# A decoder's linear attention: seven levels of scores as products of 32 columns, two halves of a projection moved, a bank counter set back

## The chip, the cores and the metric

The kernel runs on one core of a Trainium2 chip. The metric is the device time of one execution in microseconds (us), the median of several executions. Engines by their names in the profile: PE is the matrix engine (PEld its weight loads), DVE the vector engine, ACT the scalar engine, POOL the general engine, SP the queue that issues most DMAs. SBUF is the on-chip memory; PSUM is the matrix engine's result memory, here eight banks of 128 partitions by 512 float32.

## The reference

Two layers over 512 tokens of width 1024. Each layer is FFN, mixer, FFN, with a norm ahead of each part. The mixer of the first layer is the gated linear attention (GLA) that the change touches; that of the second is a stick-breaking attention (SB).

```python
for i in range(DEPTH):                      # DEPTH = 2, D_FF = 2816
    x = x + 0.5 * swiglu(rmsnorm(x, ffn1_norm[i]), ...)
    h = rmsnorm(x, mix_norm[i])
    y = gla_mixer(h, ...) if i % 2 == 0 else sb_mixer(h, ...)
    x = x + y
    x = x + 0.5 * swiglu(rmsnorm(x, ffn2_norm[i]), ...)
return rmsnorm(x, final_norm)
```

In GLA there are 4 heads with keys of 128 and values of 256. `b` is a running sum of log gates per key channel, and within a chunk

```python
diff = b_t[:, :, :, None, :] - b_t[:, :, None, :, :]
decay = jnp.exp(jnp.where(causal[:, :, None], diff, -jnp.inf))
scores = jnp.einsum('bhtk,bhtsk,bhsk->bhts', q_t, decay, k_t)
```

The decay depends on the key channel, so the scores are no plain product of q and k.

## The kernel before, in words

**Layout.** Tokens lie along the free axis (512 columns), features on the 128 partitions. A float32 product of full precision of the projections is made of three products of split operands (`mm3`, line 63 through `mm`): each weight tile is split by ACT (line 134, high part) and DVE (line 135, low part). Attention products are plain float32: the hardware does each as two passes, and the trace shows two weight loads and two matmuls for it.

**Order of the work.** Every projection is an `Entry` in one long queue, `feed`. `feed.step(1)` emits half of an entry of type `feat` (12 matmuls of 512 columns) or a quarter of one of type `tok`; `feed.entries(n)` emits whole ones. The GLA code calls `feed.step` between its own small steps, so that the projections fill the PE while DVE and ACT prepare the next attention step. A planner (the Tile framework's scheduler) then orders each engine's instructions by its own estimate; only inside a `manual_schedule` region is the order of an engine the written one among the region's own instructions.

**Banks.** PSUM banks have four tags: `a` (2 banks), `z` (3), `t` (2), `o` (1). Products without a tag take banks in the ring `aazzztto`; `turn_` counts on over the whole program. The products that close GLA and SB (`back`) use tags a, a, z, z for their first four accumulators and z, t, t, o for the last four.

**First FFN (lines 452 to 719).** Entries ahead of number `NORMED` multiply the raw input and scale the result afterwards (lines 672 and 679, one DVE operation per entry more). Between them, four pieces of `normed_input` scale and split the input itself, and from entry `NORMED` on that normed input (`nh`, `nl`) is used. Eight pieces `sums` follow until `sums_by`.

**Start of GLA (`run`, lines 1000 to 1046).** `two_halves` emits the first two projections (queries of heads 0 and 1, in the two `a` banks), `stats_a` the row statistics, `gate_low` 16 matmuls for the low-rank gate, `stats_b` the row scaling R (four small products, a DVE copy). Only with R can the two query products leave their banks (line 749). Then come `gate_logits`, and `feed.entries(2)`: the keys of heads 0 and 1, also with tag `a`.

**Levels (lines 850 to 905).** For each head the 128 by 128 score block of each of the four token tiles is built in S from a diagonal and seven levels B = 64, 32, ..., 1. `prepare(B)` makes from b a tile e (four DVE operations, lines 868 to 872, one exponential on ACT): in each group of 2B columns the first B hold keys with decay to the group's middle, the last B queries. Per level four products (128 weight columns, 96 for B = 32, 64 for B = 64; 64 moving columns) give all pairs, and a predicated copy with a mask (line 897, 64 columns for each of four tiles) puts the valid ones into S. A further product of k and q with 128 columns times the identity gives the diagonal (line 884). After each level one `feed.step`.

**Output (lines 907 to 989).** Transposed keys, three state products, S and state times values (`ps_o`), a square sum over the head's 256 values (`ps_on`, lines 967 to 969), a norm, and in `close` the product with the gate, split into `oh` and `ol` for `back`. The output of head h runs inside the levels of head h+1.

Of the kernel before, what the change touches and what calls it, by code (L numbers as in the profile page):

```python
# [10 lines left out]
F32 = mybir.dt.float32  # L11
F32R = mybir.dt.float32r
# [13 lines left out]
EPS = 1e-6  # L26
LEVELS = (64, 32, 16, 8, 4, 2, 1)
NEG = -1.0e30


@with_exitstack
def decoder(ctx: ExitStack, tc: tile.TileContext, a: dict, out: bass.AP):
# [29 lines left out]
    def mm(ps, l, r, first, last):  # L62
        st["pe"] = nc.tensor.matmul(ps, l, r, start=first, stop=last).ins  # L63
# [370 lines left out]
    def new_norm():  # L434
        st["h"], st["l"] = st["nh"], st["nl"]
# [16 lines left out]
    class FFN:  # L452
# [10 lines left out]
        def __init__(self, wg, wu, wd, gi, nxt, first=False, last=False):  # L463
            self.gi, self.normed, self.first = gi, False, first
            self.evac_g_, self.evac_u_ = self.evac_g, lambda ps: self.evac_u(ps, 0)
            if first:
                self.NORMED = 7
            self.defer, self.gates = [], []
# [253 lines left out]
    class GLA:  # L722
        def __init__(self, w_in, w_gk2, b_gk, og, w_out, nxt):
            self.w_in, self.w_gk2, self.b_gk, self.og = w_in, w_gk2, b_gk, og
            self.defer = []
            self.q, self.k, self.b, self.v = [None] * 4, [None] * 4, [None] * 4, []
            self.gn, self.on, self.hs = [None] * KD, [None] * KD, []
            chunks = [Chunk(cols(w_in, c * 256, 256), KD, 256) for c in range(4)]

            def qk(h):  # L730
                feat(chunks[h // 2], h % 2, lambda ps: self.evac_q(h, ps), "a", self.defer if h < 2 else None)

            def kk(h):
                feat(chunks[2 + h // 2], h % 2, lambda ps: self.evac_k(h, ps), "a")

            qk(0), qk(1), kk(0), kk(1), qk(2), qk(3), kk(2), kk(3)
            for c in range(4):
                tok(w_in, 1024 + c * 256, lambda i, ps, c=c: self.evac_v(c, i, ps), "a")
                ch = Chunk(cols(w_in, 2048 + c * 256, 256), KD, 256)
                for f in range(2):  # L740
                    feat(ch, f, lambda ps, j=2 * c + f: self.evac_g(j, ps), "a")
            back(w_out, 0, KD, self.hs, 1.0, nxt, late=2, tags=("a", "a", "z", "z", "z", "t", "t", "o"))
# [43 lines left out]
        def gate_weights(self):  # L786

            gr = self.ep.tile([P, KD, 16], F32, tag="gr", bufs=1, name="gr")
            with nc.allow_non_contiguous_dma("gate columns"):
                nc.gpsimd.dma_start(gr, cols(self.w_in, 3072, 16))  # L790
            self.gs = gs = self.ep.tile([P, KD, P], F32R, tag="gs", bufs=1, name="gs")
            nc.gpsimd.memset(gs.bitcast(F32), 0.0)
            nc.scalar.copy(gs[:, :, 0:16], gr)
            nc.vector.tensor_tensor(
                out=gs[:, :, 32:48], in0=gr, in1=gs[:, :, 0:16].bitcast(F32), op=ALU.subtract
            )
            w2 = self.gp.tile([P, T], F32, tag="g", name="w2")
# [12 lines left out]
            nc.gpsimd.dma_start(lf, a["c_lvl"])  # L810
            self.lvl = self.ep.tile([P, len(LEVELS) * P // 2], U8, tag="lvl", bufs=1, name="lvl")
            nc.vector.tensor_copy(self.lvl, lf)
            self.gf = self.gp.tile([P, T], F32, tag="g", name="gf")
# [3 lines left out]
        def gate_low(self):  # L817
            self.psg = psum("ps_gk", "z")
            for k in range(KD):
                mm(self.psg, self.gs[:, k], st["h"][k], k == 0, False)  # L820
                mm(self.psg, self.gs[:, k], st["l"][k], False, k == KD - 1)

# [27 lines left out]
        def levels(self, h):  # L850


            q, k, b = self.q[h], self.k[h], self.b[h]
            H = P // 2
            self.S[h] = S = self.hp.tile([P, NT, P], F32, tag="S", bufs=3, name="S")

            def four(t):
                return t.rearrange("p (n s) -> p n s", n=NT)

            def prepare(B):  # L860
# [3 lines left out]

                e = self.ep.tile([P, T], F32, tag="e", name="e")
                (b0, b1), (e0, e1) = halves(b), halves(e)
# [7 lines left out]

            def seconds(t, B):

                return t.rearrange("p (n m two c) -> p n m two c", n=NT, two=2, c=B)[:, :, :, 1, :]

            e = prepare(LEVELS[0])
            ps = psum("ps_S", "z")  # L880
            for i in range(NT):
                s = slice(i * P, (i + 1) * P)
                mm(ps[:, s], k[:, s], q[:, s], True, True)
            nc.vector.tensor_tensor(
                out=S, in0=four(ps), in1=ident.unsqueeze(1).to_broadcast([P, NT, P]), op=ALU.mult
            )
            yield
            for li in range(len(LEVELS)):
                e1 = prepare(LEVELS[li + 1]) if li + 1 < len(LEVELS) else None
                yield  # L890
                B = LEVELS[li]
                ps = psum("ps_S", "z")[:, 0 : T // 2].rearrange("p (n m c) -> p n m c", n=NT, c=B)

                R = P - B if B >= 32 else P
                for i in range(NT):
                    mm(ps[0:R, i], e[:, i * P : i * P + R], seconds(e, B)[:, i], True, True)
                nc.vector.copy_predicated(
                    out=seconds(S.rearrange("p n s -> p (n s)"), B)[0:R],
                    mask=self.lvl[0:R, li * H : (li + 1) * H]
                    .rearrange("p (m c) -> p m c", c=B)  # L900
                    .unsqueeze(1)
                    .to_broadcast([R, NT, H // B, B]),
                    data=ps[0:R],
                )
                e = e1

        def output(self, h):
# [57 lines left out]
            nc.scalar.copy(sh, sq)  # L965
            nc.vector.tensor_tensor(out=sl, in0=sq, in1=sh.bitcast(F32), op=ALU.subtract)
            ps = psum("ps_on", "o")
            mm(ps, self.one, sh, True, False)
# [31 lines left out]
        def run(self):  # L1000
            with ExitStack() as es:
# [5 lines left out]
                self.v = [vp.tile([P, D], F32, name=f"v{i}") for i in range(NT)]  # L1007
                self.S = [None] * 4
                new_norm()
                exp_ln_tables(st["silu"])  # L1010
# [34 lines left out]
                self.close(3)  # L1045
                feed.entries(self.end + 2 - feed.pos)


    class SB:
# [139 lines left out]
        def run(self):  # L1189
            with ExitStack() as es:  # L1190
# [19 lines left out]
                for s in range(17):  # L1210
# [16 lines left out]
                    else:  # L1227
                        feed.step(n)
                feed.entries(self.end + 2 - feed.pos)


# [255 lines left out]
```

## Time and profile before

| What | Value |
|---|---|
| median of 3 runs | 1815.3 us (1815.18 to 1816.06) |
| the profiled execution's own time | 1816.56 us |
| span of the profiled execution, first to last instruction | 1814.8 us |
| PE, DVE, ACT busy | 1794.2, 1473.1, 926.2 us |
| mean granted TensorE clock | 0.998 |
| first FFN | until about 340 us |
| GLA | about 346 to 577 us |

How to read it: timeline rows give start and duration in us, engine, line, operation, output and inputs, shape (for PE weight rows by weight columns, then the moving operand), how many were merged, and in square brackets the idle time of the engine before it with what ended it. Matmuls overlap in the pipeline, so the distance between starts, not the duration, tells what one costs. Busy time by stretch has PE, PEld, DVE, ACT, POOL, each with a count, then the granted clock.

### The profile page before, as it was taken

What the parts mean: (1) busy time and instruction counts of PE and PEld (TensorE: products, weight loads), DVE (VectorE), ACT (ScalarE), POOL (GpSimd) and SP (SyncE); (2) the same over time, 40 slices, a digit from 0 to 9 for tenths busy, and PEclk for the clock granted to TensorE, in tenths of its full rate; (3) what the DMA queues carried; (4) which work ended last, traced back from release to release, by engine and by line L of the source; (5) the groups of instructions that cost most, each with busy time, mean ns of one, the idle gap of its engine ahead of it and who ended that gap; (6) DMA issues with size and microseconds to landing.
All of it is one profiled execution on the core that took longest, in us unless ns stands there. A gap on an engine that the chain in (4) does not pass through costs nothing.

```text
span 1814.8 us, 28968 instructions
## 1 busy us (share of the span) xinstructions
PE 1794.2 (99%) x11806; PEld 1640.7 (90%) x11806; DVE 1473.1 (81%) x2373; ACT 926.2 (51%) x1455; POOL 8.5 (0%) x20
## 2 busy tenths in 40 slices
PE   9999999999999999999999999999999999999998
PEld 7899999889988899999989999999888788999997
DVE  7988887776877988887898888787888779888785
ACT  6444435445554544444554444455888844444444
POOL 0000000100000000000000000000000000000000
PEclk9999999999999999999999999999999999999999
DMA  6243333212223323332233333233221223333321
GB/s 210 72 131 112 105 117 114 84 51 67 70 70 102 107 94 112 113 125 84 82 119 119 110 116 106 89 96 96 70 71 59 70 93 116 105 105 105 120 90 70
DMA packets 177608, 179.09 MB, mean 99 GB/s; under 512 B 4098, under 2 KB 167988, under 8 KB 177476
## 3 DMA queue, kind: packets, MB, share of 16 engines
q1 hardware_dynamic: 176224, 175.13, 29.9%
q8 instruction: 92, 1.51, 0.3%
q0 software_dynamic: 576, 1.05, 0.2%
q10 hardware_dynamic: 676, 1.07, 0.2%
q14 instruction: 40, 0.33, 0.1%
HBM read 175.17 MB, written 2.10 MB: 98 GB/s over the span
## 4 chain that ended last, share of the span: by engine, by line
PE 85%; DVE 8%; ACT 4%; DMA 3%; issue 1%; DVEq 0%; ACTq 0%; SPq 0%
PE ps_d L63 23%; PE ps_w L544 14%; PE ps_f L63 14%; PE ps_z L544 9%; PE ps_q L544 9%; PE ps_t L63 4%; PE ps_b L63 3%; DVE wl L135 2%; PE ps_S L63 1%; DMA raw<-in_ffn_w_up_dram 1%; PE ps_bt L63 1%; PE ps_oT L1176 1%; PE ps_z L1114 1%; DMA raw<-in_ffn_w_gate_dram 1%; ACT wh L134 1%
## 5 line engine op out<-in xcount | busy, mean ns | idle before, releaser
L135 DVE TENSOR_TENSOR wl<-raw,wh 128x1024 fp32r<-128x1024 f32 x242 | 258.2, 1068 | 50.4 <-ACT wh L134 49.7
L134 ACT CAST wh<-raw 128x1024 fp32r<-128x1024 f32 (+1 forms) x242 | 223.8, 927 | 130.0 <-PE ps_f L63 43.4
L63 PE MATMUL ps_d<-hh,wh 128*128 128x512 f32 x672 | 254.7, 379 | 0.0
L63 PE MATMUL ps_d<-hh,wl 128*128 128x512 f32 x672 | 254.7, 379 | 0.0
L63 PE MATMUL ps_d<-hl,wh 128*128 128x512 f32 x672 | 254.7, 379 | 0.0
L134 ACT CAST wh<-s 128x1024 fp32r<-128x1024 f32 x136 | 142.3, 1046 | 115.0 <-PE ps_q L544 82.0
L135 DVE TENSOR_TENSOR wl<-s,wh 128x1024 fp32r<-128x1024 f32 x136 | 165.8, 1219 | 23.9 <-ACT wh L134 22.7
L63 PE MATMUL ps_f<-xh,wh 128*128 128x512 f32 x456 | 178.7, 392 | 3.4 <-DVE x L243 1.7
L63 PE MATMUL ps_f<-xh,wl 128*128 128x512 f32 x456 | 173.8, 381 | 0.4 <-DVE wl L1366 0.4
L63 PE MATMUL ps_f<-xl,wh 128*128 128x512 f32 x456 | 173.6, 381 | 0.0
L309 DVE SCALAR_TENSOR_TENSOR x<-ps_d,x 128x512 f32<-128x512 f32 x184 | 124.6, 685 | 59.8 <-PE ps_d L63 59.7
L544 PE MATMUL ps_z<-th,wh 128*128 128x256 f32 x544 | 150.1, 276 | 0.3 <-DVE u L555 0.2
L544 PE MATMUL ps_w<-nh,wl 128*128 128x256 f32 x544 | 149.6, 275 | 0.0
L544 PE MATMUL ps_w<-nl,wh 128*128 128x256 f32 x544 | 149.6, 275 | 0.0
L544 PE MATMUL ps_z<-th,wl 128*128 128x256 f32 x544 | 149.6, 275 | 0.0
L544 PE MATMUL ps_z<-tl,wh 128*128 128x256 f32 x544 | 149.6, 275 | 0.0
L544 PE MATMUL ps_w<-nh,wh 128*128 128x256 f32 x544 | 149.5, 275 | 0.0
L134 ACT CAST wh<-rawd 128x1024 fp32r<-128x1024 f32 x84 | 88.0, 1048 | 120.4 <-PE ps_d L63 100.7
L63 PEld LDWEIGHTS ps_d<-hl,wh 128*128 128x128 f32 x672 | 127.0, 189 | 18.0
L63 PEld LDWEIGHTS ps_d<-hh,wl 128*128 128x128 f32 x672 | 127.2, 189 | 16.5
L63 PEld LDWEIGHTS ps_d<-hh,wh 128*128 128x128 f32 x672 | 127.2, 189 | 16.5
L135 DVE TENSOR_TENSOR wl<-rawd,wh 128x1024 fp32r<-128x1024 f32 x84 | 102.6, 1222 | 34.7 <-ACT wh L134 34.4
(268 smaller groups left out, 4711.0 us busy)
## 6 DMA issues: line engine op xcount, KB each, us to landing
raw<-in_ffn_w_gate_dram SPq DMA_DIRECT2D x43, 1024.0 KB, 5.1
raw<-in_ffn_w_up_dram SPq DMA_DIRECT2D x43, 1024.0 KB, 5.1
rawd<-in_ffn_w_down_dram SPq DMA_DIRECT2D x84, 512.0 KB, 3.5
raw<-in_gla_w_in_dram SPq DMA_DIRECT2D x12, 1024.0 KB, 5.3
raw<-in_sb_w_in_dram SPq DMA_DIRECT2D x16, 512.0 KB, 3.8
raw<-in_gla_w_out_dram SPq DMA_DIRECT2D x4, 1024.0 KB, 5.1
raw<-in_sb_w_in_dram SPq DMA_DIRECT2D x4, 1024.0 KB, 5.0
raw<-in_sb_w_out_dram SPq DMA_DIRECT2D x4, 1024.0 KB, 4.9
```

The lines of the kernel that those rows point to most:

```text
L63: st["pe"] = nc.tensor.matmul(ps, l, r, start=first, stop=last).ins
L134: nc.scalar.copy(h, r).ins,
L135: nc.vector.tensor_tensor(out=l, in0=r, in1=h.bitcast(F32), op=ALU.subtract).ins,
L309: nc.vector.scalar_tensor_tensor(out=x, in0=back_by(ps, 4), scalar=0.5, in1=x, op0=ALU.mult, op1=ALU.add)
L544: nc.tensor.matmul(pairs(o), l_, r_, start=first and j + n == 0, stop=j == 3 and n == 2, skip_group_check=True)
L1114: nc.tensor.matmul(o_, l_, r_, start=first, stop=last, skip_group_check=True)
L1176: nc.tensor.matmul(po[e * 64 : e * 64 + 64, j * P : T], self.v[j][:, c : c + 64], self.wt[p, e][bk][:, c0 : c0 + n], start=j == 0, stop=j ...
```

## The change

1. **Levels.** All seven `prepare` calls come first (seven e tiles in buffers of their own, one `feed.step` after each and one more), then one region of PE products in written order. Each product has 32 weight columns and writes 32 partitions of PSUM; neighbours in the order go to different groups of 32 columns of the array. Levels 64 and 32 give blocks off the diagonal (16 products a head, moving columns 64 or 32), the diagonal and levels 16 to 1 only the four 32 by 32 blocks of each tile (16 products with 32 and 80 with 16 moving columns): 112 products a head for 32.
2. **Evacuation.** The blocks off the diagonal go straight to S by three ACT copies; the rest is gathered in a tile C of 32 columns a tile by one DVE product and five predicated copies of 16 columns a tile, and four DVE copies put C on S's diagonal. S is two lasting tiles, zeroed once by POOL.
3. **First keys.** The keys of head 0 take a `z` bank; half of that entry is emitted ahead of `stats_b`, half behind the query evacuations.
4. **Ring.** `turn_` is set to 0 at the end of GLA and of SB.
5. **Smaller edits.** `NORMED` of the first FFN is 8 for 7; `output` has one more yield ahead of `ps_on`, and the steps after it change so that the same number is taken; the gate columns are made in two tiles, the masks are folded to 16 columns a level by small DVE operations, and a folded identity is made.

```diff
+FINE = LEVELS[2:]
...
             if first:
-                self.NORMED = 7
+                self.NORMED = 8
...
             def kk(h):
-                feat(chunks[2 + h // 2], h % 2, lambda ps: self.evac_k(h, ps), "a")
+                feat(chunks[2 + h // 2], h % 2, lambda ps: self.evac_k(h, ps), "a" if h else "z")
...
-            self.S[h] = S = self.hp.tile([P, NT, P], F32, tag="S", bufs=3, name="S")
+            S = self.S[h] = self.Ss[h % 2]
...
-                e = self.ep.tile([P, T], F32, tag="e", name="e")
+                e = self.ep.tile([P, T], F32, tag="le", bufs=7, name="e")
...
+            es = []
+            for B in LEVELS:
+                es.append(prepare(B))
+                yield
+            yield
+            coarse, fine = psum("ps_S", "z"), psum("ps_C", "z")
+            def tile_(ps, c0, j, l, r):
...
+                o = ps[j * 32 : j * 32 + 32, c0 : c0 + n]
...
+                nc.tensor.matmul(o, l, r, start=True, stop=True, skip_group_check=True)
+            with tc.manual_schedule(engines={mybir.EngineType.PE}):
+                for i in range(NT):
+                    c = i * P
+                    for j, (li, m, n) in enumerate(((0, 64, 64), (0, 64, 64), (1, 96, 32))):
+                        tile_(coarse, (0, 0, T // 2)[j] + i * n, j, es[li][:, c + j * 32 : c + j * 32 + 32], es[li][:, c + m : c + m + n])
+                    tile_(coarse, T // 2 + i * 32, 0, es[1][:, c : c + 32], es[1][:, c + 32 : c + 64])
+                for i in range(NT):
+                    for j in range(NT):
+                        c = slice(i * P + j * 32, i * P + j * 32 + 32)
+                        tile_(fine, i * 32, j, k[:, c], q[:, c])
+                for n, B in enumerate(FINE):
+                    for i in range(NT):
+                        for j in range(NT):
+                            c = slice(i * P + j * 32, i * P + j * 32 + 32)
+                            e = es[n + 2][:, c]
+                            r = e.rearrange("p (m two c) -> p m two c", two=2, c=B)[:, :, 1, :]
+                            tile_(fine, P + n * 64 + i * 16, j, e, r)
+            C = self.hp.tile([P, NT, 32], F32, tag="C", bufs=1, name="C")
             nc.vector.tensor_tensor(
-                out=S, in0=four(ps), in1=ident.unsqueeze(1).to_broadcast([P, NT, P]), op=ALU.mult
+                out=C,
+                in0=fine[:, 0:P].rearrange("p (n c) -> p n c", n=NT),
+                in1=self.eye.unsqueeze(1).to_broadcast([P, NT, 32]),
+                op=ALU.mult,
             )
...
-            for li in range(len(LEVELS)):
-                e1 = prepare(LEVELS[li + 1]) if li + 1 < len(LEVELS) else None
-                yield
...
-                for i in range(NT):
-                    mm(ps[0:R, i], e[:, i * P : i * P + R], seconds(e, B)[:, i], True, True)
+            for n, B in enumerate(FINE):
                 nc.vector.copy_predicated(
...
+            nc.scalar.copy(S[0:64, :, 64:P], coarse[0:64, 0 : T // 2].rearrange("p (n c) -> p n c", n=NT))
+            for m in (0, 64):
+                nc.scalar.copy(
...
+            for j in range(NT):
+                s = slice(j * 32, j * 32 + 32)
+                nc.vector.tensor_copy(S[s, :, s], C[s])
...
             nc.vector.tensor_tensor(out=sl, in0=sq, in1=sh.bitcast(F32), op=ALU.subtract)
+            yield
             ps = psum("ps_on", "o")
...
+                self.Ss = [vp.tile([P, NT, P], F32, name=f"S{i}") for i in range(2)]
+                for S in self.Ss:
+                    nc.gpsimd.memset(S, 0.0)
...
                 self.gate_low()
+                feed.step(1)
                 stats_b("t")
                 flush(self.defer)
+                feed.step(1)
                 self.gate_logits()
-                feed.entries(2)
+                feed.entries(1)
...
-                        for _ in prev:
-                            feed.step(1)
+                        for n, _ in enumerate(prev):
+                            if h < 3 or n == 0:
+                                feed.step(1)
...
                 feed.entries(self.end + 2 - feed.pos)
+                turn_[0] = 0
```

More of the change, by code (lines that the diff above doesn't have):

```diff
@@ L786, in gate_weights, with fold @@
         def gate_weights(self):
-            gr = self.ep.tile([P, KD, 16], F32, tag="gr", bufs=1, name="gr")
+            def fold(x, y):
+                nc.vector.tensor_tensor(out=x, in0=x, in1=y, op=ALU.add)
+            gr = self.ep.tile([P, KD, 16], F32, tag="e", name="gr")
             with nc.allow_non_contiguous_dma("gate columns"):
                 nc.gpsimd.dma_start(gr, cols(self.w_in, 3072, 16))
[L791 to L796, printed above, removed]
+            self.gs = []
+            for u in range(2):
+                gs = self.ep.tile([P, 4, P], F32R, tag="le", bufs=7, name="gs")
+                nc.gpsimd.memset(gs.bitcast(F32), 0.0)
+                r = gr[:, u * 4 : u * 4 + 4]
+                nc.scalar.copy(gs[:, :, 0:16], r)
+                nc.vector.tensor_tensor(
+                    out=gs[:, :, 32:48], in0=r, in1=gs[:, :, 0:16].bitcast(F32), op=ALU.subtract
+                )
+                self.gs += [gs[:, k] for k in range(4)]
             w2 = self.gp.tile([P, T], F32, tag="g", name="w2")
@@ L810, in gate_weights @@
             nc.gpsimd.dma_start(lf, a["c_lvl"])
-            self.lvl = self.ep.tile([P, len(LEVELS) * P // 2], U8, tag="lvl", bufs=1, name="lvl")
-            nc.vector.tensor_copy(self.lvl, lf)
+            n = len(FINE) * 16
+            by = lf[:, 2 * P // 2 :].rearrange("p (l j c) -> p l j c", j=NT, c=16)
+            fold(by[:, :, 0:2], by[:, :, 2:4])
+            fold(by[:, :, 0], by[:, :, 1])
+            self.lvl = self.ep.tile([P, n], U8, tag="lvl", bufs=1, name="lvl")
+            nc.vector.tensor_copy(self.lvl.rearrange("p (l c) -> p l c", c=16), by[:, :, 0])
+            ey = self.ep.tile([P, P], F32, tag="e", name="ey")
+            nc.vector.tensor_tensor(out=ey[:, 0:64], in0=ident[:, 0:64], in1=ident[:, 64:P], op=ALU.add)
+            self.eye = self.ep.tile([P, 32], F32, tag="eye", bufs=1, name="eye")
+            nc.vector.tensor_tensor(out=self.eye, in0=ey[:, 0:32], in1=ey[:, 32:64], op=ALU.add)
             self.gf = self.gp.tile([P, T], F32, tag="g", name="gf")
@@ L819, in gate_low @@
             for k in range(KD):
-                mm(self.psg, self.gs[:, k], st["h"][k], k == 0, False)
-                mm(self.psg, self.gs[:, k], st["l"][k], False, k == KD - 1)
+                mm(self.psg, self.gs[k], st["h"][k], k == 0, False)
+                mm(self.psg, self.gs[k], st["l"][k], False, k == KD - 1)
         def gate_logits(self):
@@ L853, in levels @@
             q, k, b = self.q[h], self.k[h], self.b[h]
-            H = P // 2
-            self.S[h] = S = self.hp.tile([P, NT, P], F32, tag="S", bufs=3, name="S")
-            def four(t):
-                return t.rearrange("p (n s) -> p n s", n=NT)
+            S = self.S[h] = self.Ss[h % 2]
             def prepare(B):
@@ L873, in prepare @@
                 return e
[L875 to L880, printed above, removed]
-            for i in range(NT):
-                s = slice(i * P, (i + 1) * P)
-                mm(ps[:, s], k[:, s], q[:, s], True, True)
+            es = []
[3 more added lines that the diff above has]
+            yield
@@ new lines, in levels @@
+            coarse, fine = psum("ps_S", "z"), psum("ps_C", "z")
+            def tile_(ps, c0, j, l, r):
+                n = 1
+                for d in r.shape[1:]:
+                    n *= d
+                o = ps[j * 32 : j * 32 + 32, c0 : c0 + n]
+                if len(r.shape) == 3:
+                    o = o.rearrange("p (m c) -> p m c", c=r.shape[2])
+                nc.tensor.matmul(o, l, r, start=True, stop=True, skip_group_check=True)
[16 more added lines that the diff above has]
+                            tile_(fine, P + n * 64 + i * 16, j, e, r)
@@ L884, in levels @@
+            C = self.hp.tile([P, NT, 32], F32, tag="C", bufs=1, name="C")
             nc.vector.tensor_tensor(
-                out=S, in0=four(ps), in1=ident.unsqueeze(1).to_broadcast([P, NT, P]), op=ALU.mult
-            )
-            yield
-            for li in range(len(LEVELS)):
-                e1 = prepare(LEVELS[li + 1]) if li + 1 < len(LEVELS) else None
[L890 to L895, printed above, removed]
-                    mm(ps[0:R, i], e[:, i * P : i * P + R], seconds(e, B)[:, i], True, True)
+                out=C,
+                in0=fine[:, 0:P].rearrange("p (n c) -> p n c", n=NT),
+                in1=self.eye.unsqueeze(1).to_broadcast([P, NT, 32]),
+                op=ALU.mult,
+            )
@@ L897, in levels @@
+            for n, B in enumerate(FINE):
                 nc.vector.copy_predicated(
-                    out=seconds(S.rearrange("p n s -> p (n s)"), B)[0:R],
-                    mask=self.lvl[0:R, li * H : (li + 1) * H]
+                    out=C.rearrange("p n (m two c) -> p n m two c", two=2, c=B)[:, :, :, 1, :],
+                    mask=self.lvl[:, n * 16 : n * 16 + 16]
                     .rearrange("p (m c) -> p m c", c=B)
                     .unsqueeze(1)
-                    .to_broadcast([R, NT, H // B, B]),
@@ L903, in levels @@
-                    data=ps[0:R],
-                )
-                e = e1
+                    .to_broadcast([P, NT, 16 // B, B]),
+                    data=fine[:, P + n * 64 : P + n * 64 + 64].rearrange("p (n m c) -> p n m c", n=NT, c=B),
+                )
+            nc.scalar.copy(S[0:64, :, 64:P], coarse[0:64, 0 : T // 2].rearrange("p (n c) -> p n c", n=NT))
+            for m in (0, 64):
+                nc.scalar.copy(
+                    S[m : m + 32, :, m + 32 : m + 64],
+                    coarse[m : m + 32, T // 2 : T // 2 + P].rearrange("p (n c) -> p n c", n=NT),
+                )
@@ L1229, in run @@
                 feed.entries(self.end + 2 - feed.pos)
+                turn_[0] = 0
     phases = []
```

## The prediction

> **What bounds the kernel now.** I read the page first, then busy time by stretch around GLA, then timelines.
>
> ```profile
> span 1814.8 us, 28968 instructions
> ...
> PE 1794.2 (99%) x11806; PEld 1640.7 (90%) x11806; DVE 1473.1 (81%) x2373; ACT 926.2 (51%) x1455; POOL 8.5 (0%) x20
> ```
>
> ```profile
> 45.00:55.00 10.00, 8.12 (x36) 6.47 (x36) 10.00 (x21) 8.38 (x14) 0.00 (x0) 1.00 0.00 0
> 346.00:376.00 30.00, 28.29 (x126) 22.50 (x125) 15.46 (x35) 11.51 (x18) 0.00 (x0) 0.94 0.23 76
> 376.00:410.00 34.00, 34.00 (x220) 31.06 (x219) 30.93 (x66) 12.61 (x20) 0.00 (x0) 1.00 0.27 85
> 410.00:560.00 150.00, 148.71 (x1005) 136.00 (x1004) 110.53 (x205) 76.83 (x127) 0.00 (x0) 1.00 0.20 66
> ```
>
> PE is busy 99% of the span, and within GLA's levels (376 to 560) 182.7 of 184 us: there a product that goes away shortens the run, as long as DVE keeps up. DVE has room on average (141.5 of 184), little in the first head (30.93 of 34). Two stretches differ: at 45 to 55 DVE is full and PE waits; at 346 to 376 PE waits and its granted clock falls to 0.94.
>
> **The change, part by part.** *Levels, removed.* What one level costs PE is read between two of the surrounding projection's matmuls.
>
> ```profile
> 382.65 0.38 PE L63 MATMUL ps_f<-xl,wh 128*128 128x512 f32 x1
> 382.96 0.68 PE L63 MATMUL ps_S<-e 128*64 128x64 f32 x8
> ...
> 383.89 0.38 PE L63 MATMUL ps_f<-xh,wl 128*128 128x512 f32 x1
> ...
> 386.05 0.38 PE L63 MATMUL ps_f<-xl,wh 128*128 128x512 f32 x1
> ...
> 387.18 0.38 PE L63 MATMUL ps_f<-xh,wl 128*128 128x512 f32 x1
> ...
> 389.34 0.38 PE L63 MATMUL ps_f<-xl,wh 128*128 128x512 f32 x1
> 389.56 1.00 PE L63 MATMUL ps_S<-e 128*128 128x64 f32 x8
> ...
> 390.67 0.38 PE L63 MATMUL ps_f<-xh,wl 128*128 128x512 f32 x1
> ```
>
> The projection's own pitch is 0.216 us: 387.18 and 389.34 are the second and the twelfth matmul of one step, ten pitches apart. From 389.34 to 390.67 lie two pitches and a level of 128 weight columns: 1.33 - 0.43 = 0.90 us for eight passes. The same sum gives 0.81 for the level B = 64 ahead of 383.89 and 0.70 for B = 32 ahead of 387.18. A head has five levels at 0.90, one at 0.70, one at 0.81, and the diagonal, also eight passes of 128 columns, at 0.90: 6.9 us; four heads 27.6 us.
>
> *Levels, added.* 112 products a head are 224 passes of 32 weight columns. The trace has no such pass; the nearest are the weight loads of the levels before, and SB's products in two groups of 64 columns.
>
> ```profile
> L63 PEld LDWEIGHTS ps_S<-e x224: 133/192/192, 383.0 to 519.7; 128*128 128x128 f32 x80, 128*64 128x64 f32 x16, 128*96 128x96 f32 x16
> ```
>
> ```profile
> 1447.35 0.38 PE L1161 MATMUL ps_T<-ident,r 128*128 128x128 f32 x2
> 1447.66 2.37 PE L1176 MATMUL ps_oT<-wt,w 128*64 128x512 f32 x16
> 1449.96 0.48 PE L63 MATMUL ps_b<-oh,wh 128*128 128x512 f32 x1
> ```
>
> A load of 64 columns takes 133 ns, one of 128 takes 192: 0.030 us for 32 columns. I take that as the pitch of 32-column passes within one column group; 16 moving columns are short beside it. Do passes of different groups overlap? The 16 passes of L1176 (four each with 512, 384, 256 and 128 moving columns; the row names the first shape) end within 2.30 us (1447.66 to 1449.96). A pass of 128 moving columns costs 0.11 (two in 0.38 us, one lasting 0.27), so one after another they would take 16 x 2.5 x 0.11 = 4.4 us: they run in pairs. I assume the same of four groups of 32. The busiest group has, a head, 8 passes with 64 moving columns (0.056 each, half of 0.11) and 8 with 32 for the blocks off the diagonal, 8 for the diagonal, 40 for the fine levels: 0.45 + 56 x 0.030 = 2.1 us.
>
> Going from the whole array to groups and back drains it: after the last transpose (1447.35 + 0.11) a start was due at 1447.57 and came at 1447.66. I count this 0.09 twice, 0.10 for the uncovered load on the way back (0.48 for the usual 0.38) and half as much on entry: 0.33 a head. With 0.4 for unevenness 2.8 us a head, 11.2 in all (bounds 2.4 and 3.4 a head). Gain **16.4 us** (14 to 18).
>
> *Evacuation.*
>
> ```profile
> L897 DVE COPY_PREDICATED S<-lvl,ps_S x28: 420/438/742, 384.0 to 520.1; 128x256 f32<-128x256 uint8 x20, 64x256 f32<-64x256 uint8 x4, 96x256 f32<-96x256 uint8 x4
> L884 DVE TENSOR_TENSOR S<-ps_S,ident x4: 674/682/684, 379.1 to 486.0; 128x512 f32<-128x512 f32 x4
> ```
>
> A head loses seven copies at 0.43 and one product at 0.68, 3.7 us of DVE. By the slope of the two rows (256 columns 0.43, 512 columns 0.68) one product of 128 columns, five copies of 64 and four of 128 cost 0.3 + 5 x 0.25 + 4 x 0.3 = 2.8. ACT's three copies a head, under 1.5 us, lie on an engine half idle. S is read several steps later, so I cost this at nothing; uncovered, it would be 3 us in a head.
>
> *First keys.*
>
> ```profile
> 356.70 1.13 PE L63 MATMUL ps_R<-dg,gT 128*128 128x128 f32 x8
> 359.43 0.49 PE L63 MATMUL ps_f<-xh,wh 128*128 128x512 f32 x1 [1.60 <-DVE q L749]
> 359.72 0.63 PE L63 MATMUL ps_f<-xh,wl 128*128 128x512 f32 x1
> ...
> 363.13 0.39 PE L63 MATMUL ps_f<-xh,wh 128*128 128x512 f32 x1
> ```
>
> The last of eight R passes starts at 357.56 (356.70 + 1.13 - 0.27), so the keys were due at 357.67 and start at 359.43: both `a` banks hold queries until line 749 has run. Then eight matmuls take 3.41 us (359.72 to 363.13) for 1.72: the granted clock halved behind the pause. Together 3.45 us. With a `z` bank, half of the keys (12 x 0.215 = 2.6 us) runs ahead of R and half behind it, which covers the copy of R and the two queries (2 us of DVE). Next late are the gate logits, some 2 us further down DVE and ACT; head 1's keys can fill that if the planner puts them there. Gain **3.2** (1.5 to 3.5). [...]
>
> *Ring.*
>
> ```profile
> 577.06 0.38 PE L63 MATMUL ps_f<-xh,wh 128*128 128x512 f32 x1
> 579.14 0.48 PE L63 MATMUL ps_f<-xh,wh 128*128 128x512 f32 x1 [1.70 <-DVE x L243]
> ```
>
> Behind GLA the second matmul was due at 577.28 and came at 579.14, 1.86 late. Counted through the code, the ring stands at 111 there, so the FFN's first product takes bank `o`, which `back` empties last (line 243). Set to 0, it takes the two `a` banks, empty long since. Next come the input's last tiles; 24 matmuls of first halves (5.2 us) cover them. Gain **1.8** (0 to 1.9). At SB's end the waits view has no such wait: nothing.
>
> *First FFN.*
>
> ```profile
> 53.47 0.48 PE L63 MATMUL ps_f<-nh,wh 128*128 128x512 f32 x1 [1.36 <-ACT nh L630]
> ...
> 54.69 0.48 PE L63 MATMUL ps_f<-nl,wh 128*128 128x512 f32 x1 [0.52 <-DVE nl L631]
> ...
> 58.03 0.48 PE L63 MATMUL ps_f<-nh,wl 128*128 128x512 f32 x1 [0.27 <-DVE wl L135]
> ```
>
> PE waits 2.15 us for the normed input, by starts against pitch 0.16 more each time, 2.6. One more raw entry gives DVE 24 x 0.215 = 5.2 us more, less an added operation of 0.7. But DVE is full, and the eight `sums` now share four entries for five, so some waiting may return there. Gain **2.0** (0 to 2.6).
>
> *Square sums.*
>
> ```profile
> 443.22 0.28 PE L63 MATMUL ps_t<-wh,xh 128*128 128x256 f32 x1
> 443.66 0.50 PE L63 MATMUL ps_on<-sh,one 128*128 128x512 f32 x1 [0.16 <-ACT sh L965]
> ```
>
> Due at 443.33, 0.33 late; the added yield puts a step ahead of it. Four heads: gain **1.0** (0 to 1.3).
>
> *New waits.* The block of 112 products waits for the seventh e tile, and the projections wait behind it on PE. In head 0 PE's 34 us shrink by some 4 to 30 and DVE's 30.93 by 0.9 to 30: level, so a wait of a microsecond is likely. On DVE the first `prepare` of the next head waits until the block has read its buffer (seven of seven are in use); weight splits stand behind it, made up to two entries ahead of their use. In the last head two projection halves (5.2 us) no longer lie behind `close(2)`; products of `back` on earlier heads can take their place. On POOL two more fills of 128 x 512 stand ahead of the gate columns' DMA, some 1 us of a load wanted only after the statistics; the mask folding is a few short DVE operations in that stretch. I take **2.0 us lost** (0 to 5).
>
> Sum: 16.4 + 3.2 + 1.8 + 2.0 + 1.0 - 2.0 = 22.4. The profiled execution took 1816.6 us (its span and 1.8 around it), 1.3 above the median of 1815.3. So 1794.2 for such an execution, and **1793** as the median.
>
> **The rivals.** *One pass at a time (0.14).* Four groups don't overlap as two did, or PE can't issue short passes faster than it loads: 224 x 0.030 + 0.33 = 7.05 us a head, 0.6 more than before in all. Only the other parts are left (6.0): 22.4 - 16.4 - 0.6 = 5.4, 1810. For it: no row shows four groups, or 16 moving columns. Against: L1176's pairs. [...]
>
> *Issue-bound passes, slower (0.06).* Each short pass costs what the shortest of this trace did, the 64-column level: (0.68 - 0.22)/7 = 0.066, the last lasting 0.22 or so. 224 x 0.066 + 0.33 = 15.1 us a head, 33 more than before: 1815 + 33 - 6 = 1842. It ends slower from the pitch at which four blocks take 27.6 + 6.0: (33.6 - 1.3)/896 = 0.036 us. Against it: those passes loaded 64 columns, twice as many.
>
> *Feeders late (0.12).* The products overlap, but DVE is late at each of four heads, a pause of 1.8 and as much in lost clock, as at 357.67: 4 x 3.5 = 14 lost for 2: 1805. For it: DVE's 30.93 of 34. Against: 110.5 of 150 behind it.
>
> *The block is cut (0.04).* The planner may put other matmuls between the products; each cut costs 0.33 us again, ten cuts a head 13 us: 1806.
>
> **How the numbers follow.** Forecast 0.64, rivals 0.14, 0.06, 0.12, 0.04. The bounds of the parts give the forecast 1788 to 1805. The range goes to 1810 to take in half of the first rival and both of the last: about 0.85. Faster by over 0.2% (3.6 us; smaller differences can't be told from none here): all but the slower rival and a few of the first one's cases, 0.91; same 0.03; slower 0.06.
>
> **What would show it.** Right: the tile products of a head end within 2.4 to 3.4 us; no clock under 1.00 at 346 to 376; no wait for line 243 behind GLA; less waiting for nh and nl in the first FFN; GLA shorter by some 20 us. Wrong: starts of neighbouring tile products 0.03 us or more apart, 7 us a block; PE idle ahead of the block for the e tiles; other matmuls within it; a new wait ahead of `back`.

## The result and the profile after

The changed kernel takes 1798.39 us (median of four runs, 1797.29 to 1800.27), the kernel before 1815.68 beside it (four runs, 1815.18 to 1817.24): a ratio of 0.9904, 95% interval 0.9887 to 0.9922, 17.3 us faster. The forecast was 1793.0 with a range of 1788 to 1810: the sign and the range held, and the time lies 5.4 us above the forecast.

The profiled execution took 1799.37 us for a span of 1797.6. First the page of the changed kernel, then busy time in the four stretches that the prediction read.

```profile
span 1797.6 us, 30262 instructions
...
PE 1776.5 (99%) x12446; PEld 1624.4 (90%) x12446; DVE 1466.9 (82%) x2387; ACT 927.1 (52%) x1468; POOL 9.6 (1%) x23
...
q8 instruction: 97, 1.59, 0.4%
```

```profile
45.00:55.00 10.00, 10.00 (x48) 8.77 (x47) 10.00 (x20) 7.38 (x12) 0.00 (x0) 1.00 0.00 0
346.00:376.00 30.00, 29.91 (x146) 24.51 (x145) 16.75 (x37) 11.94 (x19) 0.00 (x0) 1.00 0.30 99
376.00:410.00 34.00, 34.00 (x426) 31.41 (x425) 33.65 (x83) 18.46 (x33) 0.00 (x0) 1.00 0.21 66
410.00:560.00 150.00, 143.91 (x1484) 129.47 (x1483) 111.19 (x211) 81.99 (x140) 0.00 (x0) 0.99 0.23 75
```

The first two stretches are what the prediction asked for: PE no longer waits at 45 to 55 (10.00 for 8.12; what is left of that wait, 0.86 us, lies behind the stretch, at 57.84), hardly waits at 346 to 376 (29.91 for 28.29), and the clock there is 1.00 for 0.94. But in the levels PE, which had been busy for 148.7 of 150 us, now stands still for 6.1 of 150. The waits view of GLA (376 to 566) names it:

```profile
PE ps_C L905 <- issue: 4.5, 2, 2.3
PE ps_t L64 <- DVE gn L775: 0.9, 1, 0.9
PE ps_b L64 <- DVE on L1029: 0.4, 1, 0.4
```

No e tile is waited for. Twice PE waits inside a block of tile products "for nothing that the profile shows" (issue). The timeline of PE shows a block without that (head 2) and one with it (head 1); each row is a group of passes, 224 a block.

```profile
465.28 0.85 PE L905 MATMUL ps_S<-e 128*32 128x64 f32 x31
...
466.25 1.57 PE L905 MATMUL ps_C<-e 128*32 128x16 f32 x160
467.75 0.48 PE L64 MATMUL ps_f<-xh,wh 128*128 128x512 f32 x1
```

```profile
426.82 1.42 PE L905 MATMUL ps_C<-e 128*32 128x16 f32 x142
430.45 0.36 PE L905 MATMUL ps_C<-e 128*32 128x16 f32 x18 [2.21 <-issue]
```

Head 2's block runs from 465.28 to 467.75: 2.47 us for 224 passes, close to the busiest group's 2.1 of the sum. Head 1's stops after 206 of its 224 passes, for 2.4 us from start to start (428.05 to 430.45). Head 3's stops after 177, also for 2.4 us, and the clock is halved behind it:

```profile
504.16 1.14 PE L905 MATMUL ps_C<-e 128*32 128x16 f32 x113
507.56 0.84 PE L905 MATMUL ps_C<-e 128*32 128x16 f32 x47 [2.26 <-issue]
508.32 0.80 PE L64 MATMUL ps_f<-xh,wh 128*128 128x512 f32 x1
...
511.04 0.38 PE L64 MATMUL ps_f<-xh,wh 128*128 128x512 f32 x1
```

From 508.32 to 511.04 lie six pitches of 0.216, so 1.3 us were due and 2.7 passed.

The table splits each profiled execution at the starts of four matmuls of the timeline: the first of the input's first FFN, the gate's first (`ps_gk`), the first behind GLA's last product (`ps_f` behind `ps_b`), and the first that reads that FFN's normed input (`nh`).

| us | to the first product | first FFN, up to the gate | gate and GLA | behind GLA, to `nh` | rest | span |
|---|---|---|---|---|---|---|
| before | 8.65 | 344.05 | 224.36 | 34.96 | 1202.76 | 1814.78 |
| after | 9.20 | 342.22 | 210.02 | 33.17 | 1202.95 | 1797.56 |
| difference | +0.55 | -1.83 | -14.34 | -1.79 | +0.19 | -17.22 |

### The profile page after: what moved, and what is told of

Its sections match the earlier page's. It is cut to its first block, busy times and chain, and to the rows that moved or that the text cites. A ratio compares the mean times of both kernels' runs of the same rounds, so it can differ in the third digit from the quotient of the medians.

```text
span 1797.6 us, 30262 instructions
## 1 busy us (share of the span) xinstructions
PE 1776.5 (99%) x12446; PEld 1624.4 (90%) x12446; DVE 1466.9 (82%) x2387; ACT 927.1 (52%) x1468; POOL 9.6 (1%) x23
## 3 DMA queue, kind: packets, MB, share of 16 engines
q8 instruction: 97, 1.59, 0.4%
## 4 chain that ended last, share of the span: by engine, by line
PE 87%; DVE 7%; ACT 4%; DMA 1%; issue 1%; DVEq 0%; ACTq 0%
PE ps_d L64 24%; PE ps_w L545 15%; PE ps_f L64 14%; PE ps_z L545 10%; PE ps_q L545 10%; PE ps_t L64 4%; PE ps_b L64 4%; DVE wl L136 1%; PE ps_bt L64 1%; ACT wh L135 1%; PE ps_oT L1227 1%; PE ps_z L1165 1%; ACT l L450 1%; PE ps_T L1212 1%; DVE l L1190 1%
```

## The experiments

**Why PE pauses.** The idea comes from two numbers of the page. PE executes 12446 matmuls and as many weight loads, 24,892 instructions, and 97 packets of kind "instruction" (1.59 MB) come in on queue q8 over the run: 257 instructions for each packet of 16.4 KB. The kernel before has 23,612 and 92, again 257. (The other queue of that kind, q14, has 40 packets in both kernels, so it is q8 that follows PE.) So the program seems to be fetched 256 instructions at a time, and a block eats 448 of them in 2.4 us. Counted in PE's program (loads, matmuls and PE's semaphore instructions; the trace's records alone give numbers lower by 2 throughout, with the same distances), the last matmul ahead of head 1's pause is instruction 6339 and ahead of head 3's 8130. The distance, 1791, is one short of 7 x 256, and in head 3 the load behind that matmul had run too, so both stop at the same place modulo 256. That place is called a packet end below. The rival: the pauses come from the data of those heads.

*e1: everything shifted by half a packet.*

```
         fill(8)
+        for _ in range(64):
+            mm(idle[0:8, 0:8], filler[:, 0:8], filler[:, 0:8], True, True)
         square(0, 0)
```

> 64 tiny products (8 columns; they only touch an idle bank) at the very start, where TensorE has nothing to do yet, add 128 instructions to its program and change nothing else: every later instruction sits half a packet of 256 instructions further on. Theory (TensorE's program arrives in packets of 256 instructions, and a block of 448 short ones eats them faster than they come): the pauses of some 2.4 us inside the blocks leave heads 1 and 3; heads 0 and 2 get one of 1.5 to 2.5 us each, at about 90% and 77% of the block, head 3's block takes 2.4 to 2.6 us, head 1's (whose first packet end lies right at its start) has none or a shorter one. Rival (the pauses come from the data: an e tile, a bank, a semaphore): they stay in heads 1 and 3 at the same product. Time: within 3 us of the changed kernel either way.

Measured: 1807.74 us (four runs, 1807.7 to 1808.67); ratio to before 0.9952 (0.9937 to 0.9967). The timeline of e1, head 0, head 2 and head 3:

```profile
398.65 1.47 PE L905 MATMUL ps_C<-e 128*32 128x16 f32 x139
402.08 0.37 PE L905 MATMUL ps_C<-e 128*32 128x16 f32 x21 [1.96 <-issue]
...
474.37 1.15 PE L905 MATMUL ps_C<-e 128*32 128x16 f32 x110
477.53 0.62 PE L905 MATMUL ps_C<-e 128*32 128x16 f32 x50 [2.00 <-issue]
...
514.98 1.54 PE L905 MATMUL ps_C<-e 128*32 128x16 f32 x160
```

The pauses moved as the packets did: heads 0 and 2 have one of 2.1 to 2.2 us (start to start), at 91% and 78% of the passes; head 3 has none. Head 1 kept one of 1.9, but behind pass 142, not 206: 64 passes earlier, which are the 128 instructions. The data theory has fallen. The time missed its expectation of 3 us by far: the 64 products were not free (the first product of the FFN starts at 12.41 for 9.20), and three pauses came for two (GLA 212.24 us for 210.02). These make 5.4 of the 8.4 us between the two profiles; 1.6 more lie in the first FFN, mostly in a wait for u, and 1.4 behind GLA. That the 64 products cause those is not shown.

*e6: the changed kernel again.*

> The changed kernel, unaltered, beside the others on the same chip. Theory (the place of the packet ends in the program decides): pauses of 2.4 us at the same products of heads 1 and 3 as in its first profile, none in heads 0 and 2, 1797 to 1800. Rival (the pauses fall where other traffic happens to delay a packet): they come in other heads, or elsewhere in the blocks.

Measured: 1799.99 us (1798.47 to 1800.38), 0.9905 (0.9888 to 0.9921). Its timeline, heads 1 and 3:

```profile
427.50 1.42 PE L905 MATMUL ps_C<-e 128*32 128x16 f32 x142
431.09 0.36 PE L905 MATMUL ps_C<-e 128*32 128x16 f32 x18 [2.17 <-issue]
...
504.78 1.14 PE L905 MATMUL ps_C<-e 128*32 128x16 f32 x113
507.93 0.59 PE L905 MATMUL ps_C<-e 128*32 128x16 f32 x47 [2.01 <-issue]
```

The pauses stand behind the very same passes. In all, six profiles have twelve pauses of this kind. For each: the number of the last matmul ahead of it (behind each one numbered 194 modulo 256 a load had run too), and the time from the packet end one before it to PE's going on.

| kernel, head | behind instruction | is | from the packet end before |
|---|---|---|---|
| after, 1 and 3 | 6339, 8130 | 24 x 256 + 195, 31 x 256 + 194 | 3.51, 3.56 us |
| e6, 1 and 3 | 6339, 8130 | the same | 3.46, 3.31 |
| e8, 1 and 3 | 6339, 8130 | the same | 3.45, 3.40 |
| e7, 1 and 3 | 6338, 8130 | 24 x 256 + 194, 31 x 256 + 194 | 3.38, 3.36 |
| e1, 0, 1 and 2 | 5570, 6339, 7363 | 21 x 256 + 194, 24 x 256 + 195, 28 x 256 + 195 | 3.30, 3.31, 3.34 |
| e10, outside a block | 5570 | 21 x 256 + 194 | 5.53 |

So a pause inside a block ends some 3.4 us (3.30 to 3.56) after the packet end ahead of it, and the block has reached the next end in 1.1 to 1.4.

Was the packet held up by other transfers? The DMA view of the changed kernel around head 3's pause (503 to 509, 40 slices of 0.15 us) says no:

```profile
DMA  0000000000000300000000000000000000000300
...
q8 instruction: 2, 0.03, 1.8%
```

Nothing else moves; a packet starts at about 505.0, as PE runs dry, and PE goes on at 507.56. At head 1 a load of 1 MB ends at 427.0, just as the first packet end is passed (426.94), and the pause is as long.

*e2: the block in two pieces.* The yield that stood ahead of the block now stands in it; `fines(a, b)` holds the loops over the levels `FINE[a:b]`. The first piece has 192 PE instructions, the second 256.

```
                 es.append(prepare(B))
                 yield
-            yield
...
-                for n, B in enumerate(FINE):
...
+                fines(0, 1)
+            yield
+            with tc.manual_schedule(engines={mybir.EngineType.PE}):
+                fines(1, 5)
```

> The block of 112 products is written in two pieces, 48 (blocks off the diagonal, diagonal, level 16) and 64 (levels 8 to 1), with one step of the surrounding projection (some 5 us of long matmuls) between; the step that stood ahead of the block is the one moved, so that the number of steps is the same. Theory of the packets: at most one packet end per piece, so no pause above 0.3 us in any head, no halved clock behind it; two pauses (4.8 us) and the lost clock (1.4) go, four more changes of mode (4 x 0.33 = 1.3) come: 4 to 6 us faster than the changed kernel, 1793 to 1794.5. Rival (the pauses come from data that arrive late, or from a wait for a bank): the second piece still waits for the last e tile at the same time, one or more pauses of 2 us stay, and the time is that of the changed kernel or longer by 1.3.

Measured: 1796.52 us (1795.81 to 1798.22), 0.9891 (0.9876 to 0.9905). The timeline of head 1's pieces (the last group of the first, and the second), and what is waited for in GLA:

```profile
422.92 0.47 PE L904 MATMUL ps_C<-e 128*32 128x16 f32 x32
...
427.76 1.30 PE L904 MATMUL ps_C<-e 128*32 128x16 f32 x128
```

```profile
PE ps_s L64 <- ACT kt L980: 0.8, 1, 0.8
PE ps_b L64 <- DVE gn L775: 0.7, 1, 0.7
PE ps_t L64 <- DVE gn L775: 0.5, 1, 0.5
PE ps_b L64 <- DVE on L1034: 0.4, 1, 0.4
```

No "issue" is left, no block pauses. GLA takes 206.36 us in the profile, 3.7 less than the changed kernel, just short of the 4 to 6 expected: PE waits 1.1 us more for evacuations than before the split (2.4 for 1.3). The median, 1.9 us below the changed kernel's first one, lies above the 1793 to 1794.5 expected.

*e5: the split, with ScalarE's copies one step earlier.* The three `nc.scalar.copy` of the blocks off the diagonal stand ahead of the new yield.

> The split of e2 again, and ScalarE's three copies of the blocks off the diagonal now stand behind the first piece instead of the second, one step (5 us) earlier. In e2 TensorE still waited 0.83 us once for kt (ScalarE) and 1.2 us in two places for gn (VectorE) behind blocks. Theory (what is left are bursts of evacuation behind a block that hold up the next evacuations): the wait for kt goes, 0.5 to 1 us faster than e2, 1795.5 to 1796. Rival (the copies lie beside other work anyway and the waits come from VectorE): the same as e2, 1796.5. Against the changed kernel, run beside it: 2.5 to 5 us faster, since no block pauses.

Measured: 1796.78 us (1796.66 to 1797.93), 0.9891 (0.9876 to 0.9905); GLA 206.43 us, and the same four waits with the same lengths. The copies are not what delays kt; the rival held. Against e6, run beside it, the longest run of the split (1797.93) is shorter than the shortest of the unsplit kernel (1798.47), and the medians are 3.2 us apart. The first four runs of the same unsplit kernel had two as short as 1797.3 and 1797.4, so what the split wins is some 2 to 3 us.

*e10: the split, with another step between.* (The lines are against e2.)

```
                 es.append(prepare(B))
                 yield
+            yield
...
-                            if n == 4:
-                                feed.step(1)
```

> The split again, with another step between the pieces: the step ahead of the block stays, and the one taken away is the extra step behind the fifth level (heads 1 to 3). Theory (both splits leave at most one packet end in 3.8 us; what differs is where the evacuations of other heads fall): no pause in any block, 1795 to 1797.5; the waits for kt (0.8) and gn (1.2) move or shrink, each up to 1 us. Rival (packet ends 3.7 us apart are not enough if a long stretch of short matmuls lies between, as the transposed products do here): a pause of 0.5 us or more in a second piece, 1798 or more.

Measured: 1797.51 us (1797.02 to 1799.85), 0.9900 (0.9884 to 0.9917). No block pauses, but there is a pause two microseconds behind head 0's second piece, in ordinary products. The timeline of PE, and the DMA view of 395 to 402 (slices of 0.175 us):

```profile
399.59 0.28 PE L64 MATMUL ps_t<-wh,xh 128*128 128x256 f32 x1
401.81 0.27 PE L64 MATMUL ps_t<-wl,xh 128*128 128x256 f32 x1 [1.95 <-issue]
```

```profile
DMA  0000095768999999999999994100000000000000
...
q1 hardware_dynamic: 1040, 1.05, 47.4%
q8 instruction: 1, 0.02, 1.0%
```

The packet end before it was passed at 396.28, when a load of 1 MB had just begun; the one instruction packet starts at 399.2, as that load ends, and PE goes on 5.53 us after the packet end for 3.4 elsewhere. Neither theory named this: here, where a large load ran, spreading the block was not enough. That the load held the packet up fits the whole trace of the changed kernel, in which 32 of the 97 packets start while a load runs (the packets of q1 that lie less than 0.3 us apart, taken as one load), 21 of them in its last half microsecond. It is not always so: ahead of the second piece of head 1 in e2 a packet started 2.3 us into a load of 4.7 us, and nothing paused. A pause of this kind was seen once, and not tried by moving the load. The waits for kt and gn gave way to others of like length (gn 1.1, st 0.8, oh 0.6).

**Do the four groups overlap?** *e3: neighbours in one column group.*

```
-                for n, B in enumerate(FINE):
-                    for i in range(NT):
-                        for j in range(NT):
+                for j in range(NT):
+                    for n, B in enumerate(FINE):
+                        for i in range(NT):
```

(The loops of the diagonal are turned round in the same way.)

> The same 112 products a head; the 96 of the diagonal and of the fine levels are written with the column group as the outermost loop, so that neighbours go to the same group of 32 columns instead of the next one. Theory (neighbours in different groups overlap, four at a time; within a group a pass costs some 0.030 us): 192 passes one after another take 5.8 us, a block about 6.3 us for 2.4; the packet ends then lie 3.6 us apart and the pauses shrink to under 1 us: 4 x 3.9 = 15.6 us more, 4 to 6 us of pauses less: 1806 to 1812. Rival (the block is bound by issuing 448 instructions at 5.3 ns, whatever the group): the block still takes 2.4 us and the pauses stay; 1798.

Measured: 1807.48 us (1806.21 to 1808.48), 0.9951 (0.9935 to 0.9968). The end of head 2's block:

```profile
471.55 4.82 PE L905 MATMUL ps_C<-e 128*32 128x16 f32 x157
476.30 0.48 PE L64 MATMUL ps_f<-xh,wh 128*128 128x512 f32 x1
```

157 passes in 4.75 us are 0.030 us each, the pitch that the prediction took from the weight loads; with the groups in turn 160 took 1.50 (466.25 to 467.75). A block takes 6.18 us in each head for 2.47, and none pauses: its packet ends lie 3.36 us or more apart. The same products, in another order, make GLA 7.2 us longer (217.23), although the pauses are gone. The issue-bound rival has fallen.

**What the other parts gave.** *e4: the levels of before, all else changed.* (All parts of the diff but those within `levels`, its masks and its buffers.)

> The levels as they were before the change (eight groups of eight products of 64 to 128 columns); all other parts of the change are in: one more normed entry in the first FFN, half of the first keys ahead of the row scaling, the bank counter set to 0 after GLA and after SB, the yield ahead of the square sums with the moved steps. By the two traces these parts gave 1.8 + 3.6 + 1.8 + 1.0 = 8.2 us: 7 to 9 us faster than before, 1807 to 1809, and the levels alone the other 9 to 10 of the 17.3. Rival (the levels gave their forecast 16.4, the rest next to nothing): 1 to 2 us faster than before, 1814.

Measured: 1811.7 us (eight runs, 1809.74 to 1812.91), 0.9968 (0.9958 to 0.9979), 5.2 us faster than before by the medians: less than expected. The profiled execution is the shortest of the eight. By its stretches: first FFN 342.25, GLA 220.12, behind it 33.47, together 7.5 us less than before; the rest is 0.8 longer. From e4 to the changed kernel GLA loses 220.12 - 210.02 = 10.1 us, which is the levels' net gain; with the 6.2 that the pauses cost (below) it would be 16.3, the 16.4 of the forecast. With the block split it is 220.12 - 206.36 = 13.8.

*e8: the first keys undone.*

```
-                feat(chunks[2 + h // 2], h % 2, lambda ps: self.evac_k(h, ps), "a" if h else "z")
+                feat(chunks[2 + h // 2], h % 2, lambda ps: self.evac_k(h, ps), "a")
```

(and the two `feed.step(1)` around the statistics out, `entries(2)` for `entries(1)`.)

> Only the first keys are undone: all of them wait for an 'a' bank again, the two steps around the statistics are out, two entries behind the gate logits as before. Theory: a pause of 1.6 to 1.9 us between the row scaling and the keys and a halved clock behind it are back: 3 to 3.6 us more than the changed kernel, 1801 to 1802. Rival (what the first keys win is lost again a little later, at the gate logits or in the first levels): the pause is back but the time is within 1 us of the changed kernel.

Measured: 1803.26 us (1799.1 to 1803.63), 0.9920 (0.9905 to 0.9934), 3.3 more than e6 beside it, though one of the four runs, 1799.1, is as short as e6's. The pause is back:

```profile
356.30 0.61 PE L64 MATMUL ps_R<-dg,gT 128*128 128x128 f32 x4
358.51 0.45 PE L64 MATMUL ps_f<-xh,wh 128*128 128x512 f32 x1 [1.60 <-DVE q L750]
358.80 0.38 PE L64 MATMUL ps_f<-xh,wl 128*128 128x512 f32 x1
359.01 0.38 PE L64 MATMUL ps_f<-xl,wh 128*128 128x512 f32 x1
```

This time the clock does not halve behind it (starts 0.21 us apart; the granted clock of 346 to 376 is 1.00). Over the whole profiled execution the mean clock is 0.997 for 0.998 in e6. GLA is 3.6 us longer than in e6, somewhat under 2 of it here; 0.001 of the clock over 1800 us would be 1.8 more, an estimate from two rounded figures.

*e7: three small parts undone at once,* each read at its own place: `NORMED = 7`, no `turn_[0] = 0`, and no yield ahead of `ps_on`.

> Three parts of the change are undone, each read at its own place: the first FFN's normed entries back to 7, the bank counter no longer set to 0 after GLA and SB, the yield ahead of the square sums out again (with the step it moved). Theory: first FFN 1.8 us longer up to the gate's first product; the wait for line 243's evacuation behind GLA's end back, 1.7 to 1.8 us; ps_on late again by 0.3 us in each of three heads; in all 4.5 us more than the changed kernel, 1802 to 1804. The moved step also puts head 2's block 48 instructions earlier against the packets (two ends in it, at 3% and 60%): it may pause, up to 2 us more. Rival (the three are noise or covered): within 1 us of the changed kernel.

Measured: 1802.94 us (1801.62 to 1804.53), 0.9924 (0.9909 to 0.9938), 3.0 more than e6 for the 4.5 expected. The timeline of e7 behind GLA and in the first FFN:

```profile
562.63 0.38 PE L64 MATMUL ps_f<-xh,wh 128*128 128x512 f32 x1
564.70 0.48 PE L64 MATMUL ps_f<-xh,wh 128*128 128x512 f32 x1 [1.70 <-DVE x L244]
```

```profile
53.80 0.48 PE L64 MATMUL ps_f<-nh,wh 128*128 128x512 f32 x1 [1.36 <-ACT nh L631]
55.01 0.48 PE L64 MATMUL ps_f<-nl,wh 128*128 128x512 f32 x1 [0.51 <-DVE nl L632]
58.36 0.48 PE L64 MATMUL ps_f<-nh,wl 128*128 128x512 f32 x1 [0.27 <-DVE wl L136]
```

The ring's wait is back: the second start is 2.07 us behind the first for 0.22, 1.85 us. In the first FFN 2.14 us of waiting are back where the changed kernel has one wait of 0.86; the stretch up to the gate takes 344.92, of which some 1.1 is a wait for u near 107.5. Such a wait comes in e5 too, whose first FFN is unchanged, so it is not counted here: 1.6 for this part. GLA did not grow, it takes 208.72 for 210.02 and 209.92: the mean granted clock is 0.999 for 0.998 in both, as if head 3's pause had not halved it this time. Head 2's block has two packet ends and did not pause.

*e9: the split, without the yield ahead of the square sums.*

> The split of e2, and ahead of the square sums the added yield is out again (with the moved steps). Without pauses in the blocks the cost of this one part can be read from GLA's length. Theory of the prediction: ps_on late by 0.33 us in each of three heads, 1.0 us more than e2, 1797.5. Rival (from e7, where GLA did not get longer and only one start of ps_on was late): the wait only changes its name, another evacuation is late instead; within 0.5 us of e2, either side: 1796 to 1797.

Measured: 1798.55 us (1796.74 to 1798.94), 0.9900 (0.9885 to 0.9915); GLA takes 206.47 us for 206.36. The waits view of the whole run has the lost yield:

```profile
PE ps_on L64 <- ACT sh L1013: 1.6, 3, 1.1
...
PE ps_f L64 <- DVE wl L136: 0.9, 1, 0.9
```

1.6 us of waiting for sh came, and the waits for kt and most of those for gn went: inside GLA the wait changes its name and the sum stays, as the rival said. The extra 2 us of the median lie outside GLA, where the rest is 2.0 longer, in part behind a wait for wl; that this follows from the yield isn't shown.

## Why the prediction was right, and where it was short

- **Levels, the sum of both prices: right.** The block was put at 2.8 us a head (2.1 for the busiest group, 0.33 to enter and leave, 0.4 to spare). It takes 2.47 in head 2 and 2.54 in head 0, and some 0.2 of entry and exit. Four groups overlap (e3 is the proof), a pass in one group costs 0.030. The gain of 16.4 is there but for the pauses (e4).
- **New waits, 2.0: the step that failed.** It looked for waits on data: the seventh e tile, the weight splits, the mask. None came; data waits in GLA are 1.3 us. What came is a wait of another kind, two pauses of 2.4 us where PE runs out of instructions, and 1.4 us of halved clock behind one: about 6.2 us, more than the 5 that the term allowed at most. The prediction costed passes by engine time and asked only whether PE can issue them fast enough, not whether its program arrives as fast. GLA became 14.3 us shorter, not the some 20 that the prediction named as a sign; without these 6.2 the changed kernel's GLA would take 203.8 us, 20.6 less than before, which is the 16.4 + 3.2 + 1.0 of the sum ahead of its 2.0 for new waits. That the time fell inside the range all the same is the width of the range, not foresight of this wait.
- **First keys 3.2: right in kind.** The pause of 1.8 went and did not return elsewhere: with the part undone it is back, and GLA is longer by it (e8). How much halved clock goes with it differs from run to run: 1.7 us behind the pause before, none in e8.
- **Ring 1.8: right.** 1.79 by the table, 1.85 by e7. From the timeline of the changed kernel behind GLA:

```profile
561.44 0.38 PE L64 MATMUL ps_f<-xh,wh 128*128 128x512 f32 x1
561.66 0.38 PE L64 MATMUL ps_f<-xh,wl 128*128 128x512 f32 x1
```

- **First FFN 2.0: right.** 1.83 by the table, 1.6 by e7; what is left is one wait:

```profile
57.84 0.48 PE L64 MATMUL ps_f<-nh,wh 128*128 128x512 f32 x1 [0.86 <-ACT nh L631]
```

- **Square sums 1.0: mis-sized.** About 0.1 by e9. The lateness of ps_on was read as time won when it goes; the evacuations behind it were late by as much. That is so beside the new levels; with those of before, this part and the first keys together took 4.24 us from GLA (e4), the 3.2 and 1.0 of the sum, and no run parts the two.
- **Evacuation at nothing: held.** The new copies on DVE are as short as estimated (0.25 for 64 columns, 0.3 for 128), from the changed kernel's view of `ps_C`:

```profile
L932 DVE COPY_PREDICATED C<-lvl,ps_C x20: 218/227/315, 397.6 to 509.9; 128x64 f32<-128x64 uint8 x20
L925 DVE TENSOR_TENSOR C<-ps_C,eye x4: 281/291/292, 397.0 to 508.4; 128x128 f32<-128x128 f32 x4
```

- **The rivals.** "One pass at a time" and "issue-bound" priced 7 and 15 us a block; it is 2.5, or 4.9 and 5.1 with a pause. In e3, where most passes do go one at a time, a block takes 6.2. There a pass in a single group takes 30 ns (157 in 4.75 us); with the groups in turn 160 passes in 1.50 us are 9.4 ns apart. "Feeders late" foresaw four pauses of 1.8 us with a halved clock behind them for want of e tiles; two of 2.4 came, for want of instructions, with DVE at 33.65 of 34 in head 0 and no wait for it. "The block is cut" did not happen.

## What to carry to other kernels

Short matmuls in different column groups overlap if neighbours in the program go to different groups (a pass of 32 weight columns cost 9.4 ns here for 30 in one group), so order them that way. But count instructions too: here a block that passed two packet ends in 1.1 to 1.4 us stopped until the next packet was in, unless that had been fetched ahead (it had started 2.0 and 1.3 us before the first end), and with 3.16 us or more between the ends (over 12 ns an instruction) it did not. Long matmuls between two pieces of at most 256 instructions took the pauses out of the blocks; beside a large load one came behind a piece (e10). A pause "for issue" at the same instruction number modulo 256 in every run (194 or 195 in all twelve here) is the sign; shifting the whole program by half a packet tells it from a wait for data.

## What the runs showed of the hardware

Where a block's last packet end lies 3.16 us or more behind the one before, no block paused (e2, e3, e9, head 2 of the changed kernel at 3.58). Two blocks passed two ends 1.45 us apart without a pause, head 0 of the changed kernel and head 2 of e7 (1.48): there the first end lies within the first 6% of the block, and the packet had started 2.0 and 1.3 us before PE executed that end, so the program was being read ahead. Head 1 of e1, with its end at the same place, was not read ahead in that way: its packet started 0.8 us behind the end (435.57 and 434.75). A load of 1 MB ran there from 432.2 to 435.9, and the packet started as that load ended, as in e10. That this is the reason is not shown.

A pause of about 2 to 2.4 us may or may not halve the clock. Behind head 3's in the changed kernel six pitches took 2.7 us for 1.3 (508.32 to 511.04); behind head 1's the starts lie at 0.11 us again from the second on (430.95 and 431.06). Behind head 2's in e1 they lie 0.43 us apart (479.09 and 479.52) for 0.216. Of the other pauses there is only the mean granted clock of the profiled executions: 0.998 in e6, as in the changed kernel, 0.999 in e7 and 0.997 in e1 and e8. What decides is not settled. The runs of the changed kernel lie up to 3 us apart (1797.29 to 1800.38 in eight); the two shortest have a mean clock of 0.999, the others 0.997 or 0.998. That this is the reason is not shown.
